# Ones products ahead of the head, and conditioning rows as plain products

## The chip, the cores and the metric

The kernel runs on one core of a Trainium2 chip. The metric is the time of one execution on the device in microseconds (us), lower is better. Several runs are made and their median is taken.

The core has five engines that work side by side: TensorE (PE; matrix products, with the loading of weights as a row of its own, PEld), VectorE (DVE), ScalarE (ACT), GpSimd (POOL) and SyncE (SP), which here issues nearly all DMAs. TensorE writes to eight banks of PSUM, each 128 partitions by 512 f32 columns.

## The reference, cut to what matters

One layer of a diffusion backbone: 256 latent tokens x and 256 context tokens ctx with 2048 channels, all float32. A conditioning vector c (and a second one, c_ctx, for the context) gives shift and scale of the normed input:

```python
sh1, sc1, g1, sh2, sc2, g2 = split(silu(c) @ w_ada + b_ada, 6)
sh1c, sc1c, *_ = split(silu(c_ctx) @ w_ada + b_ada, 6)
h_l = rms_norm(x, norm1_w) * (1 + sc1) + sh1
h_c = rms_norm(ctx, norm1_w) * (1 + sc1c) + sh1c
p_l, p_c = h_l @ w_in, h_c @ w_in      # parts for two kinds of attention
```

After that come a gated linear attention and a differential attention, their merge, and an MLP with a short convolution, each with weights of its own. The change touches only what stands before `h_l` and `h_c`: the sums of squares for the two norms, and copies of silu(c) and silu(c_ctx) in a layout that VectorE can use.

## The kernel before, in words

Channels lie on the partitions (16 tiles of 128), tokens in the free dimension. A float32 matrix product is made in one of two ways. A *plain* product takes f32 operands as they are; the profile shows it as two records. A *split* product takes operands in a rounded type (F32R) and is one record; where the full precision is wanted, an operand is cut into a high and a low part and the products of the parts are added up in PSUM.

The program starts with a *head*, followed by a *sweep* of 16 steps, one for each channel tile. All of that stands inside `pin[0] = True`: each engine's instructions stay in the order in which the program states them (`kept`, `pinned`, `keep_in_program_order`). Behind the sweep the compiler places instructions by its own estimate of the times.

The head, up to L604:

- SyncE issues the loads: x and ctx (`load_x`, L438 and L439, four loads of 512 KB each), then weights of the first steps: `load_ada(0)`, `load_sweep(0)`, `load_ada(1)`, `load_sweep(1)`. The conditioning vectors, the identity and a vector of small parameters are loaded from ScalarE's queue (L377 to L379).
- ScalarE applies silu to both conditioning vectors (`ccol_s`, L451). VectorE makes a rounded copy `chi`, a rest `clo` (L456, L457), and a rounded identity `identr` (L458).
- `cond_row(s, q, b, copy)` (L469) spreads 512 channels of vector s over all partitions: for each of four column groups the vector's column, broadcast to 128 x 128, is the stationary operand, and the identity moves through it, once with `chi` and once with `clo`. So a row is eight records of 128 columns into one PSUM bank `b`. The function returns the copy from that bank into `cb` (vector c) or `cbc` (c_ctx). There are two vectors with four rows each, eight rows in all.
- `squares`, `added_squares` and `summed_squares` (L477, L487, L494) work on the four 128 x 1024 tiles of x or ctx: ScalarE squares (VectorE does one half tile of each), VectorE adds the parts of the first three tiles together, and TensorE sums over the partitions with a plain product of ones, 256 columns each: one product for each of the first three tiles, four for the last, so 14 for both streams. They add up in one bank, `ss`, which is `sweep[4]`.
- `root` (L500) takes the inverse root of these sums: three activations on ScalarE (L503 to L505), two operations on VectorE (L506, L507).
- `ada_rows(0)` (L509, 16 plain products, 32 records) and `ada_cols(0)` (L520, two transposes and three small operations) give shift and scale of channel tile 0, and `stage(0)` (L533) makes the normed, modulated tile of x and ctx with its high and low parts.

TensorE's order in the head is: six rows (four of c, two of c_ctx) as 48 records, the 14 sums, the two last rows of c_ctx, the ada rows and transposes of step 0, and then step 0 of the sweep.

The copies from the rows' banks stand as follows. On VectorE, rows 2 and 3 of c come behind the squares, and rows 2 and 3 of c_ctx just before the root. On ScalarE, rows 0 and 1 of c come behind the root, and rows 0 and 1 of c_ctx behind stage 0.

In step k of the sweep (L605), SyncE gets the loads for step k + 2; TensorE makes 12 products of 512 columns (`sweep_row`, a group for each of four token tiles) and 18 of 256 (`sweep_col`), and in between the ada rows and transposes for step k + 1 (`ROWS_AT` says behind which group). In three of the steps the ada product is made on VectorE instead (`run_dots`, which reads `cb` and `cbc`). The ada weights share 11 buffers of 512 KB (`SLOTS`), the sweep's weights four: a load waits until its buffer's last reader is done.

Of the kernel before, what the change touches and what calls it, by code (L numbers as in the profile page):

```python
# [9 lines left out]
F32 = mybir.dt.float32  # L10
F32R = mybir.dt.float32r
# [3 lines left out]
ALU = mybir.AluOpType  # L15
# [3 lines left out]
P = 128  # L19
D = 2048  # L20
T = 256
KT = D // P
# [21 lines left out]
DOTS = [0, 0, 2, 2, 2, 2, 1, 2, 2, 3, 1, 2, 2, 3]  # L44
LATE_ADA = {13: 1, 14: 2}
ROWS_AT = [4, 4, 2, 1]
GATE_ADA = [0.25] * 4 + [0.5] * 16 + [1] * 12
NRM = [(0, 0)] * 2 + [(j, j + 1) for j in range(12)] + [(12, 14), (14, 16)]

# [101 lines left out]
def layer_kernel(tc, I, out):  # L151
    nc = tc.nc
    V, S, G, PE = nc.vector, nc.scalar, nc.gpsimd, nc.tensor
    es = ExitStack()
    with es:
# [5 lines left out]
        def acc_bank(name):  # L161
            return ps.tile([P, 512], F32, tag="acc", bufs=4, name=name)

        def aux_bank(name, j=0):
            return ps.tile([P, 512], F32, tag=f"aux{j}", bufs=2, name=name)
# [3 lines left out]
        ident = cp.tile([P, P], F32, name="ident")  # L169
        bones = cp.tile([P, P], F32R, name="bones")  # L170
        ones = cp.tile([P, P], F32R, name="ones")
# [6 lines left out]
        def vcol(name, j=0, n=1):  # L178
            o = _VEC[name][0] + j
            return vec[:, o:o + n]  # L180
# [7 lines left out]
        def act_table(name, earlier):  # L188
            t = S.preload_act_table_set(name)
            for e in earlier:  # L190
                after(t, e)
            return t
# [136 lines left out]
        def spare(k, j, name):  # L329

            return hp.tile([P, 512], F32, tag=f"{'ac'[j]}{k}", name=name)
# [37 lines left out]
        with tc.tile_pool(name="first", bufs=1) as p1:  # L369
            kept = tc.keep_in_program_order  # L370

            def pinned(*args, **kw):

                return kept(PE.matmul(*args, **kw))  # L374

            ccol_s = p1.tile([P, KT, 32], F32, name="ccol_s")
# [10 lines left out]
            def x_tile(s, k):  # L387
                return X[s][k // 4][:, k % 4 * T:(k % 4 + 1) * T]
# [62 lines left out]
            silus = [kept(S.activation(ccol_s[:, :, :2], ccol, AF.Silu))]  # L451
            after(silus[0], act_table("silu_and_others", []))
            logs = kept(act_table("natural_log_exp_and_others", silus))
            identr = p1.tile([P, P], F32R, name="identr")
            chi, clo = [p1.tile([P, KT, 2], F32R, name=n) for n in ("chi", "clo")]
            kept(V.tensor_copy(chi, ccol_s[:, :, :2]))  # L456
            kept(V.tensor_tensor(clo, ccol_s[:, :, :2], chi.bitcast(F32), op=ALU.subtract))  # L457
            kept(V.tensor_copy(identr, ident))  # L458
            b1 = p1.tile([P, KT], F32, name="b1")
            nw1 = p1.tile([P, KT], F32, name="nw1")  # L460
            G.tensor_scalar(b1, vcol("b_ada", 16, 16), 1.0, None, op0=ALU.add)
# [3 lines left out]
            sweep = [acc_bank(f"sweep{j}") for j in range(4)] + [aux_bank(f"sweep{j}", 1 - j // 6) for j in range(4, 7)]  # L465
# [3 lines left out]
            def cond_row(s, q, b, copy):  # L469

                for u in range(4):
                    for i, c in enumerate((chi, clo)):
                        pinned(b[:, u * P:(u + 1) * P], c[:, 4 * q + u, s:s + 1].to_broadcast([P, P]), identr,
                               start=i == 0, stop=i == 1)
                return lambda: kept(copy((cb, cbc)[s][:, q * 512:(q + 1) * 512], b))

            def squares(s, j, us=(0, 1)):  # L477

                for u in us:
                    sq = squared[s][j][u] = spare(2 * j + u, s, "sq")  # L480
                    x = X[s][j][:, u * 512:(u + 1) * 512]
                    if j < 3 or u == 0:
                        kept(S.activation(sq, x, AF.Square))
                    else:
                        kept(V.tensor_tensor(sq, x, x, op=ALU.mult))

            def added_squares(s, j):  # L487
                sq = squared[s][j]
                kept(V.tensor_tensor(sq[0], sq[0], sq[1], op=ALU.add))
                kept(V.tensor_tensor(sq[0][:, :T], sq[0][:, :T], sq[0][:, T:], op=ALU.add))  # L490
# [3 lines left out]
            def summed_squares(s, j, o, first, last, n):  # L494

                parts = [q[:, h * T:(h + 1) * T] for q in squared[s][j] for h in range(2)][:n]
                for i, p in enumerate(parts):
                    pinned(o, ones.bitcast(F32), p, start=first and i == 0, stop=last and i == n - 1)
# [21 lines left out]
            def ada_cols(k, row):  # L520

                o = ab[:, T:]
                both = p1.tile([P, 2, 2], F32, tag="both", bufs=2, name="both")
                m = p1.tile([P, 2, 2], F32, tag="shsc", bufs=2, name="shsc")
                for u in range(2):
                    kept(PE.transpose(o[:, u * P:(u + 1) * P], row[:, u * P:(u + 1) * P], ident))
                quarters = o.rearrange("p (u g v) -> p u v g", u=2, g=4)
                kept(V.tensor_reduce(both, quarters[:, :, :2, :], axis=AX.X, op=ALU.add))
                kept(V.tensor_scalar(m[:, 1], both[:, 1], b1[:, k:k + 1], nw1[:, k:k + 1], op0=ALU.add, op1=ALU.mult))
                kept(V.tensor_scalar(m[:, 0], both[:, 0], vcol("b_ada", k), None, op0=ALU.add))  # L530
                return m

            def stage(k, m, streams=(0, 1), lows=()):  # L533

                for s in streams:
                    Y, n, (hi, lo) = (A, B)[s], "ac"[s], H[s]
                    Y.append(hp.tile([P, 2, T], F32R, tag=f"{n}{k}", name=f"{n}{k}"))
                    hi.append(Y[k][:, 1, :])
                    lo.append(Y[k][:, 0, :])
                for s in streams:  # L540
                    x = x_tile(s, k)
                    kept(V.scalar_tensor_tensor(x, x, m[:, 1, s:s + 1], z1[:, s * T:(s + 1) * T],
                                                op0=ALU.mult, op1=ALU.mult))
                    kept(S.activation(H[s][0][k], x, AF.Identity, bias=m[:, 0, s:s + 1]))
                for low in lows[:1]:
                    low()
                for s in streams:
                    kept(V.scalar_tensor_tensor(H[s][1][k], x_tile(s, k), m[:, 0, s:s + 1], H[s][0][k].bitcast(F32),
                                                op0=ALU.add, op1=ALU.subtract))
                for low in lows[1:]:  # L550
                    low()

            def sweep_splits(k, lows=None):
                n = 32 + C0
                raw = raws1.pop(k)
                return split(raw[:, :n], n, lows), split(raw[:, n:SWW], SWW - n, lows)
# [19 lines left out]

            pin[0] = True
            ss = sweep[4]
            copies = [cond_row(0, q, sweep[q], S.copy if q < 2 else V.tensor_copy) for q in range(4)]
            copies += [cond_row(1, q, sweep[5 + q], S.copy) for q in range(2)]  # L580
            for s in range(2):
                o = ss[:, s * T:(s + 1) * T]
                for j in range(2):
                    squares(s, j)
                    added_squares(s, j)
                    summed_squares(s, j, o, j == 0, False, 1)
                squares(s, 2)
                squares(s, 3)
                added_squares(s, 2)
                summed_squares(s, 2, o, False, False, 1)  # L590
                summed_squares(s, 3, o, False, True, 4)
            for c in copies[2:4]:
                c()
            copies += [cond_row(1, q, sweep[q], V.tensor_copy) for q in range(2, 4)]
            for c in copies[6:]:
                c()
            root(ss)
            for c in copies[:2]:
                c()
            row, lows = ada_rows(0), []  # L600
            nxt = sweep_splits(0, lows)
            stage(0, ada_cols(0, row), lows=lows)
            for c in copies[4:6]:
                c()  # L604
            for k in range(KT):  # L605
                ws = nxt
# [12 lines left out]
                if k + 2 in DOT_TILES:  # L619
                    m = dotted(k + 2)  # L620
                at = ROWS_AT[min(k, len(ROWS_AT) - 1)]
                steps = [lambda t=t: sweep_row(k, ws[0], t) for t in range(4)]
                steps += [lambda g=g: sweep_col(k, ws[1], g) for g in range(3)]
                for i, step in enumerate(steps):
                    if turned and i == at:
                        row = ada_rows(k + 1)
# [360 lines left out]
        with tc.tile_pool(name="diff", bufs=1) as pd:  # L987
# [99 lines left out]
            def gate_tile(j):  # L1087
                ada_next(GATE_ADA[len(gates)])
                b = acc_bank("gate")
# [57 lines left out]
        for c in range(KT):  # L1147
# [7 lines left out]
            for b, j in ((ba, c), (bb, 16 + c)):  # L1155
                t = p3.tile([P, T], F32, tag="pt", bufs=2, name="pt")
                i = added(t, b)
# [29 lines left out]
        for c in range(KT):  # L1187
            b = acc_bank("mix")
# [13 lines left out]
            i = V.scalar_tensor_tensor(x1[c], b[:, T:], adav[:, c:c + 1], xr, op0=ALU.mult, op1=ALU.add)  # L1202
# [25 lines left out]
        for k in range(KT):  # L1228
            raw = fetch(I["w_up0"][k], UPS * P)
            for j in range(UPS):  # L1230
# [3 lines left out]
                o = banks[j][:, :T + 2]  # L1234
# [10 lines left out]
        for j in range(UPS):  # L1245
            u = C[KT - 1 - j][:, 1, :]
# [8 lines left out]
        with tc.tile_pool(name="ffn", bufs=1) as pf:  # L1255
# [117 lines left out]
            for h in range(2):  # L1373
                banks.append([[acc_bank("down") if h else aux_bank("down", t) for n in range(2)] for t in range(2)])
                last = FT - 2 if h else FT
# [30 lines left out]
```

## Time and profile before

| | us |
|---|---|
| median of 3 runs | 1686.57 (1686.25 to 1690.37) |
| the profiled execution | 1686.85 |
| its span in the profile | 1684.9 |
| TensorE busy | 1667.0 (99% of the span) |
| VectorE busy | 1304.9 (77%) |
| ScalarE busy | 978.2 (58%) |
| GpSimd busy | 338.5 (20%) |

How to read it. The span runs from the first to the last instruction of one execution; the execution's own time is 1.95 us more. Times in the views are counted from the span's start. TensorE's records are pipelined and overlap, so a record is longer than the step from one record to the next, and the step is what counts. A slice of the page is a fortieth of the span (42.1 us), with the busy share in tenths. "The chain" is followed back from the last instruction: at each step to what released it, or to the instruction before it on its engine. In a timeline or a chain, a row gives the start, the length, the engine and the line; `out<-in` are the tiles, `xN` is a count of instructions that follow one another, and the brackets hold the idle time before with what ended it. L374 is the line of the helper `pinned`, so most of TensorE's records in the head and the sweep have that line: they are told apart by their tiles. The granted clock is the share of TensorE's full clock.

### The profile page before, as it was taken

How to read it: one execution, taken by the hardware profiler on the slowest of the kernel's cores; microseconds unless marked ns; L12 is line 12 of the kernel's file. 1: busy time of each engine (PE TensorE's matmuls, PEld its weight loads, DVE VectorE, ACT ScalarE, POOL GpSimd, SP SyncE). 2: the span in 40 equal slices, each digit the busy share in tenths (PEclk: the TensorE clock that was granted, in tenths of full speed). 3: DMA queues.
4: the chain of work that ended last, by engine and by line, in shares of the span. 5: the costliest groups of instructions: out<-in, count | busy, mean ns of one | idle time of the engine just before them, and what ended most of it. 6: DMA issues, size and time to landing. Idle time of an engine off the chain costs nothing.

```text
span 1684.9 us, 28493 instructions
## 1 busy us (share of the span) xinstructions
PE 1667.0 (99%) x10038; PEld 1443.7 (86%) x10038; DVE 1304.9 (77%) x2484; ACT 978.2 (58%) x1975; POOL 338.5 (20%) x440
## 2 busy tenths in 40 slices
PE   7999999999999999999999999999999999999998
PEld 6779999998788888888888998888888888888887
DVE  4788867768787888788988797878888787755655
ACT  4334555756355777666665686666666666544443
POOL 0001213131310000001324200222222222684000
PEclk9999999999999999999999999999999999999999
DMA  9995644436554555688887666677777676676664
GB/s 361 387 379 188 229 150 141 142 109 197 191 188 151 178 192 191 205 292 271 272 261 255 184 200 218 228 226 239 237 237 235 228 238 214 208 219 209 216 194 143
DMA packets 110831, 370.82 MB, mean 220 GB/s; under 512 B 14432, under 2 KB 19552, under 8 KB 110688
## 3 DMA queue, kind: packets, MB, share of 16 engines
q1 hardware_dynamic: 102112, 362.51, 65.3%
q10 hardware_dynamic: 4032, 4.37, 0.8%
q0 software_dynamic: 4544, 2.14, 0.6%
q8 instruction: 78, 1.28, 0.3%
q14 instruction: 65, 0.53, 0.1%
HBM read 364.73 MB, written 2.10 MB: 218 GB/s over the span
## 4 chain that ended last, share of the span: by engine, by line
PE 97%; DVE 2%; DMA 1%; ACT 0%; issue 0%; DVEq 0%; ACTq 0%
PE down L1358 14%; PE upg L268 9%; PE upv L268 9%; PE gate L268 7%; PE sweep L374 6%; PE upv L270 5%; PE upg L270 5%; PE gate L270 4%; PE mix L268 4%; PE mix L270 2%; PE pgb L268 2%; PE pga L268 2%; PE dk L339 2%; PE dvb L285 2%; PE dk L338 2%; PE dvb L284 2%
## 5 line engine op out<-in xcount | busy, mean ns | idle before, releaser
L210 ACT CAST whi<-wraw 128x512 fp32r<-128x512 f32 (+2 forms) x1004 | 606.1, 608 | 388.9 <-DVE wlo L217 111.3
L217 DVE TENSOR_TENSOR wlo<-wraw,whi 128x512 fp32r<-128x512 f32 (+2 forms) x932 | 635.7, 690 | 221.9 <-ACT whi L210 209.4
L268 PE MATMUL upg<-a,whi 128*128 128x512 f32 x656 | 229.0, 391 | 0.0
L268 PE MATMUL upv<-a,whi 128*128 128x512 f32 x656 | 229.0, 391 | 0.0
L1358 PE MATMUL down<-whi,g 128*128 128x512 f32 x704 | 216.9, 389 | 0.0
L270 PE MATMUL upv<-a,wlo 128*128 128x256 f32 x656 | 182.8, 280 | 0.0
L270 PE MATMUL upg<-a,wlo 128*128 128x256 f32 x656 | 182.6, 280 | 0.0
L268 PE MATMUL gate<-a,whi 128*128 128x512 f32 x512 | 179.8, 397 | 0.0
L217 POOL TENSOR_TENSOR wlo<-wraw,whi 128x512 fp32r<-128x512 f32 x72 | 100.8, 1400 | 387.9 <-ACT whi L210 383.6
L362 DVE CUSTOM_DVE_ANT_0 araw<-araw,cb 128x1024 f32<-128x1024 f32 x128 | 162.4, 1271 | 14.5 <-DMA araw<-in_w_ada 14.5
L1358 PEld LDWEIGHTS down<-whi,g 128*128 128x128 f32 x704 | 132.1, 188 | 27.5
L268 PEld LDWEIGHTS upv<-a,whi 128*128 128x128 f32 x656 | 122.4, 187 | 26.6
L268 PEld LDWEIGHTS upg<-a,whi 128*128 128x128 f32 x656 | 122.4, 187 | 26.5
L270 PE MATMUL gate<-a,wlo 128*128 128x256 f32 x512 | 139.9, 283 | 0.0
L1358 PE MATMUL down<-wlo,g 128*128 128x512 f32 x352 | 136.9, 389 | 0.0
L270 PEld LDWEIGHTS upv<-a,wlo 128*128 128x128 f32 x656 | 123.9, 189 | 0.5
L270 PEld LDWEIGHTS upg<-a,wlo 128*128 128x128 f32 x656 | 123.9, 189 | 0.5
L268 PEld LDWEIGHTS gate<-a,whi 128*128 128x128 f32 x512 | 94.3, 188 | 19.6 <-issue 0.7
L270 PEld LDWEIGHTS gate<-a,wlo 128*128 128x128 f32 x512 | 96.4, 188 | 5.7 <-issue 1.8
L268 PE MATMUL mix<-a,whi 128*128 128x512 f32 x256 | 88.8, 396 | 0.0
L1358 PEld LDWEIGHTS down<-wlo,g 128*128 128x128 f32 x352 | 66.1, 188 | 13.6
L1331 POOL DMA_DIRECT2D row<-turned x128 | 69.5, 550 | 27.3 <-DVE turned L1327 15.1
(364 smaller groups left out, 3455.3 us busy)
## 6 DMA issues: line engine op xcount, KB each, us to landing
wraw<-in_w_up SPq DMA_DIRECT2D x164, 512.0 KB, 4.6
araw<-in_w_ada SPq DMA_DIRECT2D x128, 512.0 KB, 5.0
wraw<-in_w_down SPq DMA_DIRECT2D x88, 512.0 KB, 4.3
wraw<-in_w_gate SPq DMA_DIRECT2D x64, 512.0 KB, 4.2
wraw<-in_w_in SPq DMA_DIRECT2D x58, 512.0 KB, 4.1
ada<-in_w_ad SPq DMA_DIRECT2D x52, 512.0 KB, 8.4
wraw<-in_w_proj SPq DMA_DIRECT2D x32, 512.0 KB, 4.9
wraw<-in_w_out SPq DMA_DIRECT2D x32, 512.0 KB, 5.0
```

Of the source, the lines that this page charges most:

```text
L210: copied[0] = S.copy(hi[:, :n], raw)
L217: i = e.tensor_tensor(lo[:, :n], raw, hi[:, :n].bitcast(F32), op=ALU.subtract)
L268: i = PE.matmul(b.rearrange("p (a b) -> p a b", a=2), whi[:, sl], acts[k], start=first, stop=last)
L270: i = PE.matmul(b[:, T:], wlo[:, sl], acts[k][:, 1, :], start=False, stop=last)
L284: PE.matmul(o, lo[k][:, ts], whi[:, sl], start=False, stop=False)
L285: return PE.matmul(o, hi[k][:, ts], wlo[:, sl], start=False, stop=last)
L338: PE.matmul(o, whi[:, sl], lo[k], start=False, stop=False)
L339: i = PE.matmul(o, wlo[:, sl], hi[k], start=False, stop=last and j == 1)
L362: i = V.tensor_tensor_reduce(raw, raw, cb[:, q * 1024:(q + 1) * 1024], 1.0, 0.0, op0=ALU.mult, op1=ALU.add, accum_out=ada2[:, j, q:q + 1])
L374: return kept(PE.matmul(*args, **kw))
L1331: nc.gpsimd.dma_start(to[32 * (q % 4):32 * (q % 4 + 1), :, 32 * p:32 * (p + 1)], turned[32 * p:32 * (p + 1), :, 32 * q:32 * (q + 1)])
L1358: i = PE.matmul(banks[h][t][n], g[:, a, ts], w[n][b], start=k == 0 and (a, b) == (1, 0), stop=k == FT - 1 and b == 1)
```

## The change

- A constant `WARM = 14`: fourteen F32R products of the tile of ones with itself, 512 columns each (the moving operand is broadcast four times), stand first in TensorE's order. They write into the bank `ss`; the sums of squares overwrite them later, and nothing reads them.
- `cond_row` uses plain products: the column of `ccol_s` and the f32 identity, one product for each column group. `chi`, `clo` and `identr` and their three operations on VectorE are gone.
- The rows' places: rows 0 and 1 of c go ahead of the sums; rows 2 and 3 of c and rows 0 and 1 of c_ctx stand between the sums (`fillers`, behind the tiles (0, 0), (0, 1), (0, 2) and (1, 0)); rows 2 and 3 of c_ctx stand behind the transposes of step 0.
- The sums of a stream are stated tile by tile: VectorE's additions of tile 2 now precede its square of half of tile 3.
- The copies: rows 2 and 3 of c (VectorE) and rows 0 and 1 of c (ScalarE) ahead of the root; row 2 of c_ctx on ScalarE ahead of stage 0; row 3 and rows 0 and 1 of c_ctx on ScalarE behind stage 0.

```diff
+WARM = 14
...
-            identr = p1.tile([P, P], F32R, name="identr")
-            chi, clo = [p1.tile([P, KT, 2], F32R, name=n) for n in ("chi", "clo")]
-            kept(V.tensor_copy(chi, ccol_s[:, :, :2]))
-            kept(V.tensor_tensor(clo, ccol_s[:, :, :2], chi.bitcast(F32), op=ALU.subtract))
-            kept(V.tensor_copy(identr, ident))
...
                 for u in range(4):
-                    for i, c in enumerate((chi, clo)):
-                        pinned(b[:, u * P:(u + 1) * P], c[:, 4 * q + u, s:s + 1].to_broadcast([P, P]), identr,
-                               start=i == 0, stop=i == 1)
+                    pinned(b[:, u * P:(u + 1) * P], ccol_s[:, 4 * q + u, s:s + 1].to_broadcast([P, P]), ident,
+                           start=True, stop=True)
...
             ss = sweep[4]
-            copies = [cond_row(0, q, sweep[q], S.copy if q < 2 else V.tensor_copy) for q in range(4)]
-            copies += [cond_row(1, q, sweep[5 + q], S.copy) for q in range(2)]
+            for _ in range(WARM):
+                pinned(ss.rearrange("p (a b) -> p a b", a=4), ones, ones.unsqueeze(1).to_broadcast([P, 4, P]), start=True, stop=True)
+            copies = [cond_row(0, q, sweep[q], S.copy) for q in range(2)]
+            fillers = {(0, 0): (0, 2, 2, V.tensor_copy), (0, 1): (0, 3, 3, V.tensor_copy),
+                       (0, 2): (1, 0, 5, S.copy), (1, 0): (1, 1, 6, S.copy)}
             for s in range(2):
                 o = ss[:, s * T:(s + 1) * T]
-                for j in range(2):
+                for j in range(4):
                     squares(s, j)
-                    added_squares(s, j)
-                    summed_squares(s, j, o, j == 0, False, 1)
-                squares(s, 2)
-                squares(s, 3)
-                added_squares(s, 2)
-                summed_squares(s, 2, o, False, False, 1)
-                summed_squares(s, 3, o, False, True, 4)
-            for c in copies[2:4]:
-                c()
-            copies += [cond_row(1, q, sweep[q], V.tensor_copy) for q in range(2, 4)]
-            for c in copies[6:]:
+                    if j < 3:
+                        added_squares(s, j)
+                    summed_squares(s, j, o, j == 0, j == 3, 1 if j < 3 else 4)
+                    if (s, j) in fillers:
+                        c, q, b, copy = fillers[s, j]
+                        copies.append(cond_row(c, q, sweep[b], copy))
+            for c in copies[2:4] + copies[:2]:
                 c()
             root(ss)
-            for c in copies[:2]:
-                c()
             row, lows = ada_rows(0), []
             nxt = sweep_splits(0, lows)
-            stage(0, ada_cols(0, row), lows=lows)
-            for c in copies[4:6]:
+            m = ada_cols(0, row)
+            last = [cond_row(1, q, sweep[q], S.copy) for q in range(2, 4)]
+            last[0]()
+            stage(0, m, lows=lows)
+            for c in last[1:] + copies[4:]:
                 c()
```

## The prediction

> **What bounds the kernel now.** I read the page first (slices and chain), then the chain in order of time for the first 42 us and for short stretches of it, and last the stretches of the clock and of the DMAs. From the page:
>
> ```profile
> span 1684.9 us, 28493 instructions
> ...
> PE   7999999999999999999999999999999999999998
> ...
> PE 97%; DVE 2%; DMA 1%; ACT 0%; issue 0%; DVEq 0%; ACTq 0%
> ```
>
> TensorE is the bound in every slice, so a microsecond saved on its path in the head stays saved, unless a later stage starts to wait. One slice stands out: the first (42 us) is at 7 tenths, and the change lies wholly in it. Its chain (start, length):
>
> ```profile
> 1.18 5.12 DMA ident<-in_ident
> ...
> 6.32 0.24 DVE identr L458
> ...
> 6.60 20.48 PE sweep L374 x92
> 27.09 1.91 PE ab L374 x32
> ...
> 29.44 0.45 PE ab L526 x2
> ...
> 29.99 0.19 DVE both L528
> ...
> 31.69 4.55 PE sweep L374 x12
> 36.24 1.86 PE ab L374 x32
> ```
>
> TensorE does nothing until the identity has landed and is cast. Then it alone sets the time for 20.5 us with 92 records: 64 of conditioning rows (eight rows of four column groups, a high and a low part each) and 28 of the 14 sums of squares (a plain f32 product shows as two records). How fast these run is the point. The chain cut to single kinds of record:
>
> ```profile
> 6.60 10.29 PE sweep L374 x47
> ...
> 18.07 2.99 PE sweep L374 x7
> ...
> 21.47 3.45 PE sweep L374 x16
> ...
> 25.35 1.62 PE sweep L374 x15
> ...
> 32.48 2.59 PE sweep L374 x6
> ...
> 41.97 1.86 PE sweep L374 x8
> ```
>
> Length by count is the step from one record to the next. A 128-column record of a row takes 10.29 / 47 = 0.22 us up to 16.9 us, and 1.62 / 15 = 0.11 after 25. A 256-column record of the sums takes 2.99 / 7 = 0.427 around 19 us and 3.45 / 16 = 0.216 from 21.5 on. A 512-column product of the sweep takes 0.43 around 33 us and 0.233 around 43. So the same work takes twice as long in two places: from the start to about 21.4 us, and around 33 us. The stretches:
>
> ```profile
> 6.60:16.90 10.30, 10.30 (x48) 1.00 1.02 408
> 17.91:21.32 3.41, 3.41 (x10) 1.00 1.03 408
> ...
> 28.15:31.56 3.41, 1.24 (x18) 1.00 1.02 406
> 31.56:34.97 3.41, 3.28 (x8) 0.50 1.03 408
> ```
>
> The columns behind the length are TensorE's busy time (records), granted clock, DMA share and GB/s. The clock column shows 0.50 for the second place. For the first it reads 1.00 though the steps are doubled: I trust the steps. The second place comes right behind a stretch in which TensorE was busy for 1.24 of 3.41 us.
>
> **The change part by part.** The sum is made for the profiled execution, which took 1686.85 us (span 1684.9), 0.3 over the median of 1686.57; what I take off the one I take off the other.
>
> *The fourteen products of ones* need only the tile of ones. From VectorE's timeline:
>
> ```profile
> 0.84 0.17 DVE L174 MEMSET ones<- 128x128 f32 x1 [0.84 <-PEq L1396]
> ```
>
> So they can start at about 1.05 us, where TensorE now idles until 6.60. All slow, they take 14 x 0.427 = 5.98 us and end at 7.0, sooner if the clock rises on the way. The identity lands at 6.30 and its cast (0.24) is gone, so the rows could start at 6.35: at worst the ones cost 0.7 us, and the next step hides that.
>
> Does the clock rise? 10.3 us of row products did not raise it, though the busy column shows no gap; some 4.5 us of sums, from 16.9, did. In the sums one record follows the other at the pace of a slow 512-column product (0.427), and the array streams; a row's record takes 0.22 for a quarter of those columns, so half of its step goes to something else, its weights I think. The products of ones have 512 columns: they are like the sums. [...]
>
> *Rows as plain products.* Instead of two records per 128 columns with a rounded identity there is one plain product, again two records. The nearest full-size rows are plain f32 transposes of 128 columns; the other end is the 256-column record of the sums.
>
> ```profile
> 513.42 0.66 PE pT L1072 x6
> ```
>
> These step by 0.11 us. So a row of eight records costs from 8 x 0.11 = 0.88 us (as now, when fast) to 8 x 0.216 = 1.73. I take 0.88, the row of the same shape. Below that there is no reason: each record still loads its weights. [...]
>
> *The order up to the root.* Two rows go ahead of the sums, four between them. What the sums wait for and what waits for them, from the timelines of VectorE and ScalarE:
>
> ```profile
> 8.47 0.42 DVE L490 TENSOR_TENSOR sq<-sq 128x256 f32<-128x256 f32 x1
> ...
> 15.60 0.42 DVE L490 TENSOR_TENSOR sq<-sq 128x256 f32<-128x256 f32 x1
> ...
> 25.39 0.69 ACT L503 ACTIVATE z<-sweep,epsb 128x512 f32<-128x512 f32 x1 [10.49 <-PE sweep L374]
> ...
> 26.77 0.63 ACT L505 ACTIVATE zt<-z 128x512 f32<-128x512 f32 x1
> ...
> 27.12 0.69 DVE L475 COPY cbc<-sweep 128x512 f32<-128x512 f32 x1 [0.20 <-PE sweep L374]
> ...
> 28.44 0.69 DVE L507 SCALAR_TENSOR_TENSOR z<-zt,z 128x512 f32<-128x512 f32 x1
> ```
>
> The first summand is ready at 8.89; the first two rows take 6.35 to 8.1 (8.8 if the ones end late). From 8.9 TensorE has 28 x 0.216 = 6.05 us of sums and 4 x 0.88 = 3.52 of rows: done at 18.5. Nothing on the way is late: VectorE's squares and additions end at 16.0 now, are the same work in another order, and the last four products begin at 18.5 - 1.7 = 16.8. The root starts 0.2 later, at 18.7 instead of 25.39. From there to the end of L507 it takes 3.74 us now; 0.4 of it VectorE still copies a row (to 27.81) after the root's last activation (27.40), and that copy now comes earlier. I take 3.4: 22.1. The two copies that ScalarE had behind the root move ahead of it, into its 10.49 us of waiting.
>
> The ada rows of step 0 (1.9 us) follow the sums, 18.5 to 20.4. Of their weights the last quarter comes last (its issue, and the time to landing):
>
> ```profile
> L346 SPq DMA_DIRECT2D ada<-in_w_ad x1: 328/328/328, 9.1 to 9.1; - x1
> ...
> DMA to landing us min/median/max: 10.3/10.3/10.3
> ```
>
> It lands at 19.4; its products come at 19.9. The row's copy follows the root's last activation, and the transposes end at 21.6; the reduction that was at 29.99, 0.86 behind L507, now follows it at 22.15. From there to the first sweep product it was 1.70 us: 23.85 instead of 31.69, so 7.84 earlier.
>
> *The last two rows* now stand on TensorE between the transposes and that product, 21.6 to 23.4: the 1.8 us idle there (29.89 to 31.69) hide them. The copy that ScalarE gets ahead of stage 0 follows the first of them and ends by 23.2, if it takes what VectorE's 512-column copy does (0.69): about when stage 0's activation is due, half a microsecond ahead of that product. The copies after it push ScalarE's next casts by about 0.5 us, and those are needed a whole step later. The filled gap also keeps TensorE busy, so the slow stretch at the sweep's start goes: 12 products take 2.8 us instead of 4.5, and the second ada rows come at 26.8 instead of 36.24: 9.4 us ahead.
>
> *What is late next: the loads.* The DMAs run full (408 GB/s) until 35 us, then wait for buffers that TensorE frees. The stretches, the last load for step 2 (issue, landing), and the ada rows of steps 2 and 4:
>
> ```profile
> 35.00:40.00 5.00, 1.00 0.83 280
> 40.00:45.00 5.00, 1.00 0.97 357
> 45.00:50.00 5.00, 1.00 0.94 313
> 50.00:55.00 5.00, 1.00 0.92 331
> ...
> L346 SPq DMA_DIRECT2D ada<-in_w_ad x1: 328/328/328, 27.7 to 27.7; - x1
> ...
> DMA to landing us min/median/max: 6.7/6.7/6.7
> ...
> 43.99 1.93 PE L374 MATMUL ab<-ada,ccol_s 128*32 128x256 f32 x32
> ...
> 56.93 1.93 PE L374 MATMUL ab<-ada,ccol_s 128*32 128x256 f32 x32
> ```
>
> That load lands at 34.4, behind a full queue, so it will not come sooner. TensorE would begin there at 43.99 - 9.4 = 34.6: just in time. From it to the last quarter for step 4 the queue holds ten loads of 128x1024 f32 (0.524 MB) and two of 128x896 (0.459): 6.16 MB, 15.1 us at 408 GB/s, so 49.5. TensorE would begin those rows at 56.93 - 9.4 = 47.5 and need that quarter 1.4 later: 0.6 us of waiting. Step 5, reckoned the same way, adds 0.2, step 6 nothing. So 0.8 us go back, and 9.4 - 0.8 = 8.6 us are left.
>
> **The rivals.** *The loads do not catch up.* If the 4.3 us that the DMAs lost from 35 to 55 us, (128 + 51 + 95 + 77) / 408 x 5, stay lost, the gain is 8.6 - 4.3 = 4.3: 1682.3. Against it: buffers come free earlier with everything else. *The clock is late, or falls again.* If the ones do not raise it and plain products do, 4.5 us after their start (as now), it is slow until 11.5 us: the two first rows end at 10.6 and about 2.1 us are lost: 1680.1. If it falls again behind the weakest stretch of the new order (20.4 to 23.85, about 2.2 of 3.4 us busy), the sweep's start loses 1.6: 1679.6. For: 1.24 us of 3.41 was too little above; against: 2.2 is nearly twice that. [...] *Plain rows at the dear end,* 1.73 each: the two first end at 9.8 and the sums with four more at 22.8, and the two behind the transposes at 29.4, which leaves a gain near 3.9: 1682.7. *Slower:* the work behind the head's pinned stage is placed by the compiler from its own times, and another order there could make TensorE wait. The longest wait that it has from 131 us on:
>
> ```profile
> PE dq L268 <- DVE osq L312: 2.1, 1, 2.1
> ```
>
> To lose the 8.6, and 0.3% (5.1 us, about what a measurement of this kernel can tell from no change) more, takes 13.7 us of such waits, over six times this one: 1691.7 or above. That the change does nothing has no place: the head's records are the chain.
>
> **How the numbers follow.** Forecast 0.66, late or falling clock 0.15, loads 0.08, dear rows 0.07, slower 0.04. The first two are faster, and 2 in 100 of the next two at their edge: 0.83; 0.13 within 0.3%, 0.04 slower. Time: 1686.57 - 8.6 = 1678.0. The range runs from a gain of 11 (the order behind the head falls 2.4 us better) to the dear rows: 1675.5 to 1682.7.
>
> **What would show it.** Right: ones from about 1.1 us; rows from 6.4 in steps of 0.11; the root near 18.7; the first sweep product near 23.9, at a clock of 1.00; the second ada rows near 26.8; waits of TensorE for ada loads at 47 to 57 us, under 1 us in all; the sweep's end over 8 us earlier. Wrong: steps of 0.2 us in the rows after 8 us, a clock of 0.50 behind 23 us, waits for loads of several us, or new waits behind the sweep.

## The result and the profile after

The changed kernel took 1680.40 us (median of 6 runs, 1679.43 to 1680.91), beside 1687.01 us (6 runs, 1686.25 to 1690.37) for the kernel before on the same chip. The ratio is 0.9957 with a 95% interval of 0.9944 to 0.997: 7.3 us faster, with 5.1 to 9.4 open; the medians differ by 6.6. The forecast was 1678.0, with a range of 1675.5 to 1682.7.

The profiled execution took 1679.91 us, of which 1677.6 are the span. From the page of the changed kernel, the lines that answer to the first three shown of before:

```profile
span 1677.6 us, 28522 instructions
...
PE   9999999999999999999999999999999999999998
...
PE 95%; DMA 2%; DVE 2%; ACT 1%; issue 0%; DVEq 0%; SPq 0%; ACTq 0%
```

The first slice of TensorE went from 7 tenths to 9. The shares of the chain say little here: a second execution of the kernel before (below) has the changed kernel's 95% for TensorE and 2% for the DMAs too. The head on TensorE's timeline (start, length, operation, count, and idle time before it):

```profile
1.06 5.16 PE L375 MATMUL sweep<-ones 128*128 128x512 f32 x14 [1.06 <-DVE ones L175]
6.32 2.02 PE L375 MATMUL sweep<-ident,ccol_s 128*128 128x128 f32 x16
8.79 0.48 PE L375 MATMUL sweep<-sq,ones 128*128 128x256 f32 x1 [0.45 <-DVE sq L485]
```

The ones fill what was idle, the two first rows follow at the fast pace (16 records in 2.02 us), and TensorE then waits 0.45 us for the first summand. From there the chain of the head, in order of time (start, length, what):

```profile
8.79 9.90 PE sweep L375 x60
18.69 0.02 issue
18.71 0.70 ACT z L498
...
22.09 0.18 DVE both L523
22.27 0.06 issue
22.33 0.51 ACT whi L211
22.84 0.48 ACT cbc L470
23.32 0.42 ACT a L539
23.74 0.04 issue
23.78 3.42 PE sweep L375 x12
27.20 1.86 PE ab L375 x32
```

The root starts at 18.71 instead of 25.39, the first sweep product at 23.78 instead of 31.69, and the second ada rows at 27.20 instead of 36.24. One thing is new: ahead of the first product the chain now runs through ScalarE's cast of a sweep weight (whi) and the copy of a row (cbc). From ScalarE's timeline:

```profile
21.80 1.03 ACT L211 CAST whi<-wraw 128x512 fp32r<-128x512 f32 x2 [0.82 <-DMA wraw<-in_w_sw]
```

The cast waited 0.82 us for its weights, so a load has reached this place; it costs next to nothing yet, as VectorE's input to stage 0 was ready at 23.18 and the activation that needs it began at 23.22. In the slower head ScalarE's casts had ended 0.8 us ahead of that activation, and its copies of c_ctx stood behind it. The granted clock around that place (length, TensorE busy, clock, DMA share, GB/s):

```profile
21.50:23.80 2.30, 1.78 (x17) 1.00 1.02 406
23.80:27.20 3.40, 3.40 (x16) 1.00 1.03 409
```

The last two rows fill the gap, and the clock stays at 1.00 where the execution of before had 0.50. Now the DMAs, the same stretch of the changed kernel and then of the kernel before:

```profile
35.00:55.00 20.00, 1.00 1.03 407
```

```profile
35.00:55.00 20.00, 1.00 0.92 320
```

The loads caught up: they ran full for 20 us longer. They were still late at two places. From the waits of the changed kernel up to 131 us (total, times, longest):

```profile
PEld ab L375 <- DMA ada<-in_w_ad: 1.1, 2, 0.6
```

How far the gain got is read at the last ada rows of the sweep, in the changed kernel and then in the kernel before:

```profile
115.86 1.93 PE L375 MATMUL ab<-ada,ccol_s 128*32 128x256 f32 x32
```

```profile
124.39 1.93 PE L374 MATMUL ab<-ada,ccol_s 128*32 128x256 f32 x32
```

The lead was 36.24 - 27.20 = 9.04 us at the second ada rows and is 8.53 here, so the loads took back 0.51. The spans differ by 1684.9 - 1677.6 = 7.3, so 1.2 us were lost behind the sweep in this execution: 0.4 near 156 us on work that had waited for a load, and 0.83 at one wait of the score products, behind the sweep, for VectorE. That wait stands in the last brackets of TensorE's timeline, changed kernel and then before:

```profile
441.57 0.71 PE L863 MATMUL sc<-e 64*128 64x128 f32 x8 [1.26 <-DVE e L895]
```

```profile
448.86 0.71 PE L868 MATMUL sc<-e 64*128 64x128 f32 x8 [0.43 <-DVE e L900]
```

No engine has another order of instructions behind the head, so the program there is the same. Below, "step 14" is the start of the ada rows just shown, and "the rest" is the span less that start.

### The profile page after: what moved, and what is told of

The parts are those of the page before. It is cut to its first block, busy times and chain, and to the rows that moved or that the text cites. A ratio compares the mean times of both kernels' runs of the same rounds, so it can differ in the third digit from the quotient of the medians.

```text
span 1677.6 us, 28522 instructions
## 1 busy us (share of the span) xinstructions
PE 1664.8 (99%) x10052; PEld 1439.8 (86%) x10052; DVE 1303.0 (78%) x2479; ACT 978.6 (58%) x1977; POOL 340.0 (20%) x440
## 4 chain that ended last, share of the span: by engine, by line
PE 95%; DMA 2%; DVE 2%; ACT 1%; issue 0%; DVEq 0%; SPq 0%; ACTq 0%
PE down L1353 14%; PE upg L269 9%; PE upv L269 9%; PE gate L269 7%; PE upv L271 5%; PE upg L271 5%; PE sweep L375 5%; PE gate L271 4%; PE mix L269 4%; PE mix L271 2%; PE pgb L269 2%; PE pga L269 2%; PE dk L340 2%; PE dvb L286 2%; PE dk L339 2%; PE dvb L285 2%
```

## The experiments

The theory that the expectations test: the gain is made in the head. By this theory, TensorE's clock rises only under products whose steps are full of streaming columns (in the kernel before it rose under the sums, at 0.427 us a record, and not under the rows, at 0.22), so the ones raise it before the conditioning rows start; the rows then cost half (0.11 us a record), and the filled gap ahead of the sweep keeps it up. Rivals: any back-to-back products raise the clock; the plain form of the rows is what counts; the new order alone does it; and, for the end of the gain, TensorE and not the loads is the bound behind the head. The first five kernels take the change apart, the others look at what the head is worth and at what varies from one execution to the next. In a ratio the kernel before is always the divisor.

### Without the products of ones

```
-WARM = 14
+WARM = 0
```

> The changed kernel without its fourteen products of ones. Theory (what raises the clock is a stretch of about 3.4 us in which columns stream through the array): the plain rows stream, so they raise it themselves, but only 3.4 to 6.8 us after their start at 6.3: until about 11.4 us the steps are double (0.22 us per row record, 0.43 per record of the sums). The first sum starts near 9.9 instead of 8.8, the root 1.1 to 2.7 us later than 18.7 (middle 1.9); half a microsecond of that disappears in the waits for ada loads, so the sweep ends about 1.4 us later than with the ones and the time is 1 to 2 us above the changed kernel. Rival (the ones bring nothing, the rows' new form and places bring it all): root at 18.7, the same time as the changed kernel.

Measured: 1679.85 us (median of 5 runs), ratio 0.9962 (0.9949 to 0.9974). Two short stretches of the chain, start, length and count:

```profile
6.60 3.33 PE sweep L375 x14
...
10.47 0.88 PE sweep L375 x7
```

A stretch holds the whole length of its last record, which is longer than a step, so length by count is a little high: 0.24 us for the first rows (0.21 from start to start) and 0.126 for the later ones (0.11). The step halves at 10.0 us: here the plain rows raised the clock themselves, 3.4 us after their start at 6.60. The root starts at 19.91, 1.2 us later than with the ones, and step 14 is at 116.55, 0.69 later. The time is not above the changed kernel's, so that half of the expectation missed: what the head loses without the ones is less than the runs can tell.

### The ones in products of 128 columns

```
-WARM = 14
+WARM = 28
...
-                pinned(ss.rearrange("p (a b) -> p a b", a=4), ones, ones.unsqueeze(1).to_broadcast([P, 4, P]), start=True, stop=True)
+                pinned(ss[:, :P], ones, ones, start=True, stop=True)
```

> The changed kernel with 28 products of ones of 128 columns in place of 14 of 512: the same 6 us of slow TensorE time without a gap, but each step is half weights. Theory (streaming columns raise the clock): it stays low until the plain rows have run for 3.4 to 6.8 us; rows start near 7.0 and the root is 1.5 to 3.3 us later than 18.7, the time 1.5 to 2.5 us above the changed kernel. Rival (sustained products of any shape raise it): doubled steps end at 4.3 to 7.9 us, the root is at 18.7 to 19.0 and the time is the changed kernel's.

Measured: 1682.81 us (11 runs), ratio 0.9975 (0.9966 to 0.9984). The chain in three stretches:

```profile
1.06 5.81 PE sweep L375 x26
...
7.08 3.31 PE sweep L375 x15
...
11.24 1.06 PE sweep L375 x7
```

The 28 small products run at 5.81 / 26 = 0.22 us from first to last, as long a stretch as the fourteen large ones, and leave the clock where it was: the rows behind them start slow as well (3.31 / 15 = 0.22). It rose only at 11.5 us, 4.4 us after the plain rows had begun, and the root was at 20.86. The outcome is the one that the theory expected, and "any back-to-back products" falls: with products of 512 columns in the same 6 us the clock rose inside the stretch (up at 4.7 and at 6.0 us in two profiles of the changed kernel), with products of 128 it did not. That half of each small step is weights is the author's estimate, from a step of 0.213 us beside a quarter of 0.427; no view shows what a step is filled with.

### The rows in their old form, in the new places, behind the ones

```
+            identr = p1.tile([P, P], F32R, name="identr")
+            chi, clo = [p1.tile([P, KT, 2], F32R, name=n) for n in ("chi", "clo")]
...
-                    pinned(b[:, u * P:(u + 1) * P], ccol_s[:, 4 * q + u, s:s + 1].to_broadcast([P, P]), ident,
-                           start=True, stop=True)
+                    for i, c in enumerate((chi, clo)):
+                        pinned(b[:, u * P:(u + 1) * P], c[:, 4 * q + u, s:s + 1].to_broadcast([P, P]), identr,
+                               start=i == 0, stop=i == 1)
```

> The changed kernel with the rows in their old form (rounded identity, high and low part), in the new places and behind the ones. Theory (the plain form costs and brings nothing by itself, as both have eight records of 0.11 us; once high, the clock is held also by half-filled steps, as it was at 25 to 28 us before): rows from 6.6, the root at 18.7, clock high throughout, time within 0.3 us of the changed kernel. Rival (the half-filled steps let the clock fall): doubled steps for 3.4 us somewhere between 8 and 19 us, the root 1 to 2 us later.

Measured: 1680.16 us (5 runs), ratio 0.9963 (0.9951 to 0.9976); root 18.77, step 14 115.87. TensorE from the first summand to the root:

```profile
8.80:18.50 9.70, 9.65 (x60) 1.00 1.02 409
```

The same 60 records in the same 9.7 us as the changed kernel's (9.90 with the last one's length). With the clock up the plain form brought nothing here, and rows of high and low parts, 10.3 us of which had not raised the clock in the kernel before, stood between the sums of these 9.7 us without a fall.

### The ones alone, in the kernel before

```
             ss = sweep[4]
+            for _ in range(14):
+                pinned(ss.rearrange("p (a b) -> p a b", a=4), ones, ones.unsqueeze(1).to_broadcast([P, 4, P]), start=True, stop=True)
```

> The kernel before with only the fourteen products of ones put ahead. Theory: the clock rises at 4 to 7 us; 48 row records at 0.11 us from 6.6 to about 11.9, sums until 18.0 (the data allow 16.9), root near 18.2, that is 7.2 us earlier than before; the two last rows then stand ahead of the ada rows and ScalarE's two copies behind the root: first sweep product near 24.4. The gap ahead of it stays empty, so the clock may fall there as before (1.6 us). Time 0 to 1.7 us above the changed kernel, 4.5 to 6.5 below the one before. Rival (half-filled row steps for 5 us let the clock fall): doubled steps from about 10 us, root near 21, time 2 to 4 us above the changed kernel.

Measured: 1681.37 us (6 runs), ratio 0.9975 (0.9962 to 0.9987); by the medians 5.8 us faster, by the ratio 4.2 (2.2 to 6.4). Three stretches of the chain, and the clock behind the start of the sweep:

```profile
7.15 4.91 PE sweep L374 x44
...
12.29 5.76 PE sweep L374 x26
...
24.80 5.00 PE sweep L374 x12
```

```profile
25.90:29.20 3.30, 3.30 (x9) 0.50 1.04 412
```

Rows at 0.11, sums at 5.76 / 26 = 0.22, both at the full clock from the start, root at 18.52: the ones alone bring the whole gain up to the root. Then the gap ahead of the sweep is empty, the clock falls at 25.8 us for 3.4, and the twelve products take 5.00 us instead of 3.42. Step 14 is at 117.92, 2.1 us behind the changed kernel's. A second profile was taken to see whether that fall belongs to this order:

> The kernel before with only the products of ones ahead, a second profile. Theory: the rows and sums are fast again (root near 18.5); whether the clock falls in the gap ahead of the sweep (it did, at 25.8 us) is a matter of phase, so it may stay high here, and then the sweep's end is near 132.4 instead of 134.0. Rival (the empty gap always lets it fall): 134.0 again.

It took 1684.23 us, and it fell again at the same place; step 14 was at 118.14:

```profile
25.90:29.20 3.30, 3.30 (x9) 0.50 1.03 409
```

### The new order alone

The edit is that of the rows in their old form, above, and

```
-WARM = 14
+WARM = 0
```

> The new order alone: no products of ones, rows in their old form (rounded identity, high and low part) in the new places. Theory (only steps filled with streaming columns raise the clock; a row's old record fills half of its step): rows from 6.6 at 0.21 us per record, the mix of sums and rows is about two thirds full and may or may not do, the ten records of sums in a row surely do; the clock rises between 13 and 21 us, the root starts between 21 and 25 us, and as the gap ahead of the sweep is filled the clock stays up after it. Time 1681.5 to 1685. Rival (the new order is what matters, whatever the rows are): the root near 20 as without ones, the time within 0.5 us of that run.

Measured: 1686.88 us (12 runs), ratio 0.9997 (0.9989 to 1.0005): no gain that can be measured, where 1681.5 to 1685 was expected of the theory. Stretches of the chain, then a stretch of TensorE's timeline, then ScalarE's timeline at the root:

```profile
6.72 3.25 PE sweep L375 x14
...
10.40 2.35 PE sweep L375 x9
```

```profile
17.88 2.90 PE L375 MATMUL sweep<-sq,ones 128*128 128x256 f32 x10
```

```profile
24.30 0.69 ACT L504 ACTIVATE z<-sweep,epsb 128x512 f32<-128x512 f32 x1 [8.26 <-PE sweep L375]
```

Rows and sums stay slow (0.23 and 2.35 / 9 = 0.26 for a mix of both) up to 18.9 us, 1.1 us after the ten records of sums shown had begun; the root is 1.1 us earlier than before's 25.39. So sums alone were not needed: the 3.41 us that ended with the rise (on such windows see the last section) held eight records of a row beside sums, and the 3.41 us ahead of them, with eleven, left the clock low. Step 14 was at 120.87, some 3 us ahead of the kernel before in four profiles (below), but the profiled execution was also the fastest of the twelve (1684.92). Whether the other eleven lost the clock somewhere that this one kept it isn't known, and stays open. What does follow: moving the rows is not where the measured gain is from.

### Four rows fewer

```
-                        copies.append(cond_row(c, q, sweep[b], copy))
+                        copies.append(lambda c=c, q=q, copy=copy: kept(copy((cb, cbc)[c][:, q * 512:(q + 1) * 512], sweep[q % 2])))
-            for c in copies[2:4] + copies[:2]:
+            for c in copies[2:] + copies[:2]:
...
-            for c in last[1:] + copies[4:]:
+            for c in last[1:]:
```

The second part moves the copies of rows 0 and 1 of c_ctx from behind stage 0 to a place ahead of the root.

> The changed kernel without the four rows between the sums: TensorE makes four of the eight rows, and the copies of the others read the banks of rows 0 and 1 of c, ahead of the root. Theory (behind the root the loads are the bound now: the sweep's first weights land at 21.8 us, and the ada weights of steps 4 and 5 land behind TensorE): the sums end at 16.8 and the root starts near 17.0, 1.7 us earlier, but the first sweep product stays at 23.6 to 23.8 and the sweep's end and the time stay within 0.3 us. Rival (TensorE's own work is still the bound of the head): everything behind the root comes 1.7 us earlier, the sweep ends 1.7 us earlier and the time falls by 1.7 us.

Measured: 1680.77 us (6 runs), ratio 0.9961 (0.995 to 0.9973); step 14 116.13. The root did not come earlier (18.77), and ScalarE's timeline says why:

```profile
16.74 1.18 ACT L588 COPY cbc<-sweep 128x512 f32<-128x512 f32 x2 [1.66 <-DVE cb L588]
```

Its copies now read the same two banks as VectorE's and wait 1.66 us for them, ahead of the root. The experiment made a new wait in place of the work that it left out, and tells nothing about what four rows are worth. It was made again without the copies:

### Four rows and their copies left out

```
-                        copies.append(cond_row(c, q, sweep[b], copy))
+                        G.memset((cb, cbc)[c][:, q * 512:(q + 1) * 512], 1.0)
...
-            for c in copies[2:4] + copies[:2]:
+            for c in copies:
...
-            for c in last[1:] + copies[4:]:
+            for c in last[1:]:
```

> The changed kernel without the four rows between the sums and without their copies: TensorE makes four of the eight rows, and the places of the others in cb and cbc hold ones, set by GpSimd at the start. (In four_rows the copies, which shared two banks, held the root until 18.8; here no copy stands there.) Theory (behind the root the loads are the bound now): the sums end at 16.8 and the root starts near 17.0 instead of 18.7; the last ada weights of step 0 land at 19.4 to 19.6 and the sweep's first weights at 20.7 to 21.8, so the first sweep product comes 0 to 1 us earlier than 23.8; the ada rows of steps 4 and 5 wait for their loads for as much longer, and the sweep's end stays at 131.7 to 132.3. Rival (TensorE's own work is still the bound of the head): the sweep's end comes 1.4 to 1.7 us earlier, near 130.4, and so does the program's.

Measured: 1680.16 us (5 runs), ratio 0.9955 (0.9941 to 0.9969). The root came at 18.04 and not at 17.0, because VectorE was late with the last sums; the first sweep product was at 23.20 and the second ada rows at 26.45, 0.68 us ahead of the changed kernel (27.13 on the same timeline). From TensorE's timeline:

```profile
15.57 2.43 PE L375 MATMUL sweep<-sq,ones 128*128 128x256 f32 x10 [0.57 <-DVE sq L485]
...
49.27 0.64 PE L375 MATMUL ab<-ada,ccol_s 128*32 128x256 f32 x8 [0.36 <-DMA ada<-in_w_ad]
```

And from its waits between 40 and 64 us:

```profile
PEld ab L375 <- DMA ada<-in_w_ad: 1.6, 2, 0.8
```

The last quarter of step 4's weights makes TensorE wait again, 1.6 us in all instead of 1.1; of the lead of 0.68 us, 0.14 was left at step 5 and nothing at step 6, and step 14 is at 115.91 (115.86 in the changed kernel). The 0.68 us taken off TensorE in the head were given back to the loads in full: in this run they are the next bound there.

### The same kernels again

One more profile of the changed kernel and three more of the kernel before, with no edit, for what varies between executions of one program.

> The changed kernel unchanged, one more profile. Theory (what was lost between the sweep's end and the end of the program, 1.2 us, comes from waits in the linear attention that differ from one execution to the next): the head and the sweep repeat within 0.3 us, apart from where the clock rises (4.5 to 8 us), and the loss behind the sweep is another one, 0 to 4 us, at the same place (score products waiting for VectorE near 440 us). Rival (the loss is fixed by the earlier arrival): again 1.1 to 1.4 us.

> The kernel before unchanged, one more profile. Theory: doubled steps from 6.6 until 20 to 24 us and again for 3.4 us around the sweep's start, whichever the phase; the sweep's last product at 140 to 142 us; the wait of the score products near 449 us differs from the 0.4 us of the first profile. Rival (these waits are fixed by the program): 0.4 us again and the span within 0.2 us of 1684.9.

> The kernel before, a third profile. Theory (the windows of the clock run freely, so how long the head is slow and whether the clock falls at the sweep's start is drawn anew in each execution): the clock rises between 20 and 24 us and falls in some executions at 28 to 33 us for 3.4 us, the sweep's end at 138.5 to 141.5. Rival (it is fixed): one of the two pairs seen, 21.3 with a fall or 20.2 without.

> The kernel before, a fourth profile; as for the third. With the four, the mean of the sweep's end should lie between 138.9 and 140.5, and the mean saving at that place against the changed kernel's 131.9 between 7.0 and 8.5 us.

| Execution | time | clock up at | root | sweep's start | step 14 | the rest |
|---|---|---|---|---|---|---|
| before, shown above | 1686.85 | 21.3 | 25.39 | falls | 124.39 | 1560.5 |
| before, second | 1686.69 | 20.2 | 24.91 | stays | 122.77 | 1562.0 |
| before, third | 1689.57 | 21.4 | 25.49 | falls | 124.46 | 1563.1 |
| before, fourth | 1689.79 | 21.0 | 25.36 | falls | 124.22 | 1563.6 |
| changed, shown above | 1679.91 | 4.7 | 18.71 | stays | 115.86 | 1561.7 |
| changed, second | 1679.03 | 6.0 | 18.73 | stays | 115.81 | 1560.9 |

The second profile of the kernel before has the weak stretch ahead of the sweep and no fall behind it:

```profile
28.20:31.50 3.30, 1.01 (x11) 1.00 1.03 410
31.60:35.00 3.40, 3.40 (x21) 1.00 1.03 410
```

Its chain there:

```profile
31.20 3.41 PE sweep L374 x12
```

The third has the fall at the sweep's start, and one more far behind it:

```profile
31.60:35.00 3.40, 3.22 (x8) 0.51 1.02 407
461.80:465.10 3.30, 3.30 (x13) 0.50 0.00 0
```

So the clock at the sweep's start is a draw in the kernel before: three falls in four (the last section measures what goes with a fall). The mean of step 14 over the four is 123.96, and 115.84 over the two of the changed kernel: the head is worth 8.1 us, not 8.5. The rest varies from 1560.5 to 1564.3 us over all fourteen profiles of this study; the five highest of them (the third and fourth of before, the ones of 128 columns, the second of the ones alone, and the rows left out) are the five in which the clock fell once between 445 and 465 us.

## Why the prediction was right, and what was off

*The order of the steps held.* Ones from 1.06 us (forecast 1.05), ended at 6.2 (at most 7.0); rows from 6.32 at 0.11 us a record; first summand 8.79 (8.89); root 18.71 (18.7); first sweep product 23.78 (23.85). Each is within 0.15 us. The clock's part of it is shown by the experiments: in every kernel with large ones or plain rows it is up by 11.5 us, with neither it is not up until 18.9.

*What raises the clock.* The prediction read from the steps of before that 10.3 us of row records did not raise it and some 4.5 us of sums did, and set the products of ones beside the sums. The 128-column ones show directly that the kind of product matters here: 5.8 us of them, one behind the other without a gap, left the clock low, while the 512-column ones had it up at 4.7 us and, in a second profile of the same program, at 6.0. Why a small product's step counts for less was an estimate from the length of the steps alone (0.213 us beside a quarter of 0.427). The time to the rise is not fixed either: it came 3.4 us after the start of the plain rows without the ones, and 4.4 us after it behind the small ones. The falls lasted 3.41 us, and the last section measures what the changes of the clock have in common.

*The plain rows were not a step of their own.* The change makes them plain, and the prediction priced them at the fast pace, which held. But in the old form they cost the same behind the ones (step 14 115.87 and 115.86). Either the ones or the plain form would have done: without the ones the plain rows raised the clock 3.4 us after their start.

*The step that was mis-sized: "so the slow stretch at the sweep's start goes: 12 products take 2.8 us instead of 4.5".* They took 3.42. The execution of before whose clock did not fall took 3.41, so 2.8 isn't reached at the full clock either: the first products wait on VectorE for the low parts (0.3 and 0.2 us in the changed kernel). The term was worth 4.55 - 3.42 = 1.1 us and not 1.7 in the execution that was costed, and nothing at all in the one of four that kept its clock. (By its own terms, 23.85 and 2.8, the second ada rows would have come at 26.65 and not at 26.8.) One profiled execution was taken for the program.

*The loads.* Forecast: the last quarter for step 4 at 49.5 and 0.8 us of waiting; it landed at 49.35, and 0.51 was lost over the sweep, 0.23 at step 4 and 0.28 at step 5. The weight loader's own waits there are 1.1 us, a little over the "under 1 us in all" that was to show it right; part of them was hidden. That loads are the bound there is shown by the kernel with fewer rows.

*The sum.* 8.6 forecast, 8.5 at step 14 in the pair of profiles, 8.1 over the six, 7.3 (5.1 to 9.4) in the times. The prediction carried the head's gain to the end unchanged; in the first pair 1.2 us of it were lost behind the sweep, in the second profile of the changed kernel 0.4 (by the table), in waits that are there in the kernel before too (the score products waited 0.4, 1.3, 0.8 and 0.8 us in its four profiles, 1.3 and 0.2 in the two of the changed kernel). A microsecond saved "stays saved, unless a later stage starts to wait", it had said: right for the program, but single executions differ in such waits by about as much. Whether the remaining 0.8 us between 8.1 and 7.3 is anything can't be told: the interval holds both. Nor is it settled whether the fall near 450 us is likelier in one kernel than in the other (two of four profiles of before, none of two of the changed one).

*The rivals.* "The loads do not catch up" fell: 407 GB/s where before had 320. "The clock is late" fell at 4.7 us, and "falls again" did not come in any profile of the changed order with the gap filled, with the ones or without; it came both times where the gap was left empty behind the ones. "Dear rows" fell at 0.11 us a record. "Slower" had no wait of its size: behind the sweep TensorE's longest wait is 2.1 us in both kernels, and the longest of the score products was 1.3 us in the changed one.

## What to carry to other kernels

Read the clock from the steps of like records, not from the busy column: 10.3 us of back-to-back rows left it low here (0.22 us a record, where 0.11 is the step at the high clock), and fourteen long products on data that is there from the start, in 5.2 us that were idle anyway, raised it before the real work came. Ask then what the faster stage runs into: here the loads took the 0.68 us that was saved on top in the head. Profile the kernel before more than once before you price a clock effect: the fall at the sweep's start came in three of its four executions, so it is not a property of the program.

## What the runs showed of the hardware

In these runs some records that did not raise the clock ran on at the high clock once it was up. The rows' old records of 128 columns take 0.213 us at the low clock, where a quarter of a 512-column step (0.427) would be 0.107: by this estimate half of their step is something else. Such records did not raise it in 10.3 us (rows of the kernel before) or in 5.8 us (ones of 128 columns), while 4.9 us of the rows' ran at 0.11 us a record behind the large ones; with plain sums between them the clock stayed up for 9.7.

The times at which the clock changed are whole multiples of one length apart. In the first profile of the kernel before it rises at 21.32, falls at 31.56 and rises at 34.97 us: 3 and 1 times 3.413 us apart. In the third, the two falls (31.68 and 461.76) are 126 times 3.413 us apart. So each profile was laid out from the rise on in windows of 3.413 us. Ahead of the program's last work the fourteen profiles have ten falls, each right behind a window in which TensorE was busy for 1.22 to 1.52 us. Every other window up to 1670 us was busy for 1.63 us or more, save one of 1.49 (changed kernel, from 448.42 us), behind which the clock stayed at 1.00; why it did, the profiles do not show. One of the ten, and the window behind it, from the ones of 128 columns:

```profile
441.56:444.97 3.41, 1.42 (x14) 1.00 0.86 320
444.97:448.38 3.41, 3.41 (x13) 0.50 0.46 163
```

The draw at the sweep's start fits these windows. In the second execution of the kernel before, which did not fall, a border of two of them cut the weak stretch in two, and neither part was as weak as those ahead of the falls (1.90 and 2.63 us busy):

```profile
27.00:30.42 3.42, 1.90 (x30) 1.00 1.01 401
30.42:33.83 3.41, 2.63 (x10) 1.00 1.03 408
```

With the gap filled no window can be as weak as those: wherever 3.413 us are laid in the changed kernel's first profile between 9 and 39 us, TensorE is busy for 2.40 us of them or more. With the gap left empty behind the ones the weakest place is as weak as in the kernel before (about 1.1 us in both), and both executions fell.

TensorE was never idle for a whole window ahead of a fall: the longest gap in the ten windows was 1.4 to 2.1 us (1.81 in the first profile of the kernel before).
